# A two-layer hybrid encoder on one core: weight sums by DMA, Strassen blocks on VectorE, and a new order in the last attention head

## The chip, the core and the metric

The kernel runs on one core of a Trainium2 chip. A core has five engines with queues of their own: PE (TensorE, matrix products into PSUM, with PEld for its weight loads), DVE (VectorE), ACT (ScalarE), POOL (GpSimd) and SP (SyncE, which issues DMAs here). The metric is the device time of one execution in microseconds (us), as the median of several runs.

## The reference

768 tokens (a sequence of 512 and one of 256, stored with the shorter one first) go through two layers of width 1024 in float32. Each layer has a mixer and a feed-forward part, each followed by a residual layer norm:

```python
mix = concat([diff_attention(q, k, v, lam), sigmoid(lo) * rmsnorm(mlstm(q2, k2, v2, gates))]) @ w_out
x = layer_norm(ALPHA * x + mix)
gate, up = split(x @ w_gu)                     # 1024 -> 2 x 2816
h = gelu(conv3(gate) + conv_b) * up            # conv3 over neighbouring tokens of one sequence
x = layer_norm(ALPHA * x + h @ w_down)
```

The attention has four heads with two score matrices each, whose softmaxes are subtracted; the mLSTM part runs in both directions with four heads.

## The kernel before

**Precision.** A float32 weight or activation block is split by ACT and DVE into a rounded part (`wh`) and the rest (`wl`, DVE's subtraction in line 187), and every product is three passes on PE. Weights come by SP's queue into six raw buffers (`raw`, line 143), are cast by ACT (line 186) and DVE (line 187), and lie in twelve pairs of slots until PE has read them. The class `Weights` keeps the order of all this: `pump` casts as long as a slot is free, and `_load` issues loads.

**Order.** The code is traced in program order, and a planner writes each engine's instructions out as a fixed list: it takes what is ready by its own clock, the least number first, and `prio(n)` makes the numbers of what it holds smaller by n. A negative n lets the held work stand back. Each engine works its list off in order, so an instruction that waits holds up those behind it.

**Mixer.** Per layer come the mLSTM's inputs and gates, the values, and then per attention head `att_in` (queries and keys, line 379, then casts into `sQ`, `sK`, `kL` by ACT and DVE, lines 722 to 732) and `att` (per tile of 128 queries: scores in lines 752 and 753, the minimum by DVE, the exponential by ACT in line 758, transposes, and the product with the values). Two heads' stages are woven with other work by `weave`. Head 3 handles the sequence of 512 first (`SEQ_ORDER`), but `feat_major` projects the 256 tokens first for every head. In the stage of head 3 the work beside it is the gate projection (`lo`, line 369), its transposes (`loT`), and `split_att` (lines 819 to 825), which casts the outputs of heads 0 to 2 into `actB` for W_out: two ACT copies and two subtractions per head, on POOL for head 0 and on DVE for the others.

**W_out and the change to the FFN.** W_out runs in two column halves over six token tiles. In the second half each tile gets its layer norm: statistics (line 865), aggregate (870), two small steps on POOL (871, 872), and two passes on DVE (876, 882). The FFN's first products use the Strassen-Winograd scheme on 2 x 2 blocks (features by token halves), seven products in place of eight. `combine` (lines 896 to 909) makes the four sums of activations S1 to S4 of a token tile, for tiles 3 and 4 on POOL and for tile 5 on DVE (`VT`), and `to_strassen` transposes and casts them.

**FFN weights.** The scheme also needs four sums of weight blocks per FFN tile f: t1 = u0 + g0, t2 = u1 + t1, t3 = u1 + u0, t4 = g1 + t2. For most tiles SP loads one summand into a buffer `T` (line 152) and POOL issues a DMA that adds the other to it (line 153); four `T` buffers exist, and the next load waits until the cast of the one four earlier was made. For f = 1 and 2 (`ENG`) the raw blocks are loaded, POOL makes t1 and t3, and DVE t2 and t4 (line 164). `ff_tile` (lines 970 to 1010) runs the seven products of a tile, each in one PSUM bank (line 967); DVE reads them out in lines 983 to 999, and a bank is written again when it was read.

**Down projection and end.** `down` (line 1012) adds groups of FFN tiles into `acc`. In the last group the two column halves of a token tile follow each other, DVE adds the product (line 1034), and the layer norm and the output DMA follow (line 1050). For the very last token tiles a part of the norm's last step is done by ACT and POOL (lines 879, 880).

Of the kernel before, what the change touches and what calls it, by code (L numbers as in the profile page):

```python
# [13 lines left out]
F32 = mybir.dt.float32  # L14
# [39 lines left out]
PR_E = 50  # L54
PR_AO = -40
PR_CONV1 = -100
PR_CONV2 = -100
# [28 lines left out]
NSG = 3  # L86
NSUM = 4
ENG = (1, 2)
AT1 = 11
# [4 lines left out]
LAG1 = 2  # L94
VT = (5,)


class Weights:


# [18 lines left out]
    def block(self, src, n, dst=None):  # L119
        self.blocks.append((src, n, dst))  # L120
        for x in (src["a"], src["b"]) if isinstance(src, dict) and src["engine"] else (src,):
            if not isinstance(x, dict):
                self.uses[x] += 1

    def sum(self, layer, a, b, engine=None, over=None):

        s = {"a": a, "b": b, "engine": engine, "layer": layer, "read": False, "over": over}
        if engine is None:
            self.sums.append(s)
        return s  # L130
# [24 lines left out]
    def _value(self, src, n):  # L155
        if isinstance(src, dict):
            if "tile" not in src:

                v = [x["tile"] if isinstance(x, dict) else self.raw[x] for x in (src["a"], src["b"])]
                if isinstance(src["b"], dict) or src["over"]:  # L160
                    src["tile"] = v[1]
                else:
                    src["tile"] = self.diff_pool.tile([128, 512], F32, tag="E", name=f"E{self.n_conv}", bufs=1)
                src["engine"].tensor_tensor(out=src["tile"], in0=v[0], in1=v[1], op=ALU.add)
                for x in (src["a"], src["b"]):
                    if not isinstance(x, dict) and x != src["over"]:
                        self.uses[x] -= 1
            return src["tile"]
        return self.raw[src]

    def _conv(self, i):
        src, n, dst = self.blocks[i]
        self._load()
        v = self._value(src, n)
        if callable(dst):
            dst(v)
            self.uses[src] -= 1
            return
        if dst is None:
            h = self.hl_pool.tile([128, WCOL], F32R, tag="wh", name=f"wh{i}")[:, :n]  # L180
            l = self.hl_pool.tile([128, WCOL], F32R, tag="wl", name=f"wl{i}")[:, :n]
            self.hl[i] = (h, l)
        else:
            h, l = dst
            v = v.rearrange("p (k t) -> p k t", k=4)
        self.nc.scalar.activation(h, v, AF.Identity)  # L186
        self.nc.vector.tensor_tensor(out=l, in0=v, in1=h.bitcast(F32), op=ALU.subtract)  # L187
        if isinstance(src, dict):
            src["read"] = True
            if src["over"]:  # L190
                self.uses[src["over"]] -= 1
        else:
            self.uses[src] -= 1
        self._load()

    def pump(self):

        live = sum(1 for j in range(self.n_done, self.n_conv) if self.blocks[j][2] is None)
        while self.n_conv < len(self.blocks):
            if isinstance(self.blocks[self.n_conv][0], dict):  # L200
                self._load()
                if self.diff_pool is None or ("tile" not in self.blocks[self.n_conv][0] and not self.blocks[self.n_conv][0]["engine"]):
                    break
# [23 lines left out]
def trunk(ctx, nc, tc, d, o, depth=DEPTH):  # L227
# [59 lines left out]
    for l in range(depth):  # L287
# [19 lines left out]
        for kind, i in ffn_seq:  # L307
            if kind == "f":


                def at(w, p):
                    return d[w][l, i, :, p * 512:(p + 1) * 512]

                g0, g1 = early[i] if i in early else [W.piece(at("w_g", p), 512) for p in range(2)]
                if i in ENG:
                    u0, u1 = [W.piece(at("w_u", p), 512) for p in range(2)]
                    t1 = W.sum(l, u0, g0, G)
                    t2 = W.sum(l, u1, t1, V)
                    t3 = W.sum(l, u1, u0, G, over=u0)
                    t4 = W.sum(l, g1, t2, V)  # L320
                else:
                    u1 = W.piece(at("w_u", 1), 512)
                    t1 = W.sum(l, at("w_u", 0), at("w_g", 0))
                    t2 = W.sum(l, at("w_u", 1), t1)
                    t3 = W.sum(l, at("w_u", 1), at("w_u", 0))
                    t4 = W.sum(l, at("w_g", 1), t2)
                for src in (t1, t2, t3, t4, u1) if i in early else (g0, g1, t1, t2, t3, t4, u1):
# [42 lines left out]

    def feat_major(blocks, psA, psB):

        for ps, tok in ((psB, slice(0, SB)), (psA, slice(SB, T))):
            n = 0
# [17 lines left out]
    for l in range(depth):  # L392
# [317 lines left out]
        def att_in(h):  # L710
# [4 lines left out]
            for ui, uu in ((0, uq), (1, uk)):  # L715
                pA = P("d", f"aqkA{h}{ui}")
                pBu = pB[:, ui * 256:(ui + 1) * 256]
                feat_major(uu, pA, pBu)
                W.done(*uu)
                for ps, tk in ((pBu, slice(0, SB)), (pA, slice(SB, T))):  # L720
                    if ui == 0:
# [114 lines left out]

        weave((chain(att_in(3), att(3)), AT3, PR_A), (split_lstm(), 13 - L1 - L2, PR_LO), (chain(*[split_att(h) for h in range(3)]), 4))
        weave((split_att(3), 1))
# [28 lines left out]
        def layer_norm(t, nm, parts=1, aside=()):  # L867
            mv = sm.tile([128, 2], F32, tag="mv", name=f"mv{nm}{t}")
            rs = sm.tile([128, 1], F32, tag="rs", name=f"rs{nm}{t}")
            V.bn_aggr(mv, stats.pop(t))  # L870
            G.tensor_scalar(rs, mv[:, 1:2], EPS, 1.0, op0=ALU.add, op1=ALU.mult)
            G.tensor_tensor(out=rs, in0=rs, in1=mhalf[:, 0:1], op=ALU.pow)
# [97 lines left out]
        def ff_tile(f):  # L970
# [3 lines left out]
            c = ft.tile([128, T], F32, tag="c", name=f"c{f}")  # L974
            m1, u2, u3, u4 = (ft.tile([128, HALF], F32, tag=t, name=f"{t}_{f}") for t in ("m1", "u2", "u3", "u4"))
            lo_, hi_ = slice(0, HALF), slice(HALF, T)
            p1 = bank(f"p1_{f}")
            product(p1, A11)
# [33 lines left out]
        def down(gi):  # L1012
# [5 lines left out]
            for hf, t in ([(hf, t) for t in range(NT) for hf in range(2)] if last else [(hf, t) for hf in range(2) for t in range(NT)]):  # L1018
                if last:
                    units = us[hf]  # L1020
                elif t == 0:
                    units = [W.take() for _ in range(nf)]
                p = P("d" if last else "tu"[(hf * NT + t) % 2], f"dn{gi}{hf}{t}")
                for k, (_, wh_, wl_) in enumerate(units):
                    for i, (a, b) in enumerate(PASSES):
                        x = hm_half((f0 + k) % RING, a, t // 3)[:, (t % 3) * 128:(t % 3 + 1) * 128]
                        PE.matmul(p, x, (wh_, wl_)[b], start=k + i == 0, stop=k == nf - 1 and i == 2)  # L1027
                z = acc[:, t, hf * 512:(hf + 1) * 512]
                if t == NT - 1 and (hf or not last):
                    W.done(*(us[0] + us[1] if last else units))  # L1030
                if gi == 0:
# [3 lines left out]
                if last:  # L1035
                    half_stats(t, hf, f"b{l}")
                if last and hf:
                    final = l == depth - 1
                    parts = 4 if final and t == NT - 1 else 1
                    layer_norm(t, f"b{l}", parts, (() if t < NT - 2 else (0,) if t < NT - 1 else (3,)) if final else ())  # L1040
# [103 lines left out]
```

## Time and profile before

| | us |
|---|---|
| median of 3 runs (1808.42 to 1810.11) | 1808.9 |
| the profiled execution, its own time | 1809.26 |
| its span in the profile | 1807.5 |
| PE busy | 1770.1 |
| DVE busy | 1270.8 |
| ACT busy | 774.5 |
| POOL busy | 273.7 |

The span runs from the first to the last instruction that the profile shows; 1.8 us of the execution lie around it. The mean granted clock of TensorE is 0.997 of full speed. A matmul's recorded duration contains the pipeline behind it, so matmuls that follow each other overlap in the records, and the idle time ahead of one is what counts.

### The profile page before, as it was taken

What the parts mean: (1) busy time and instruction counts of PE and PEld (TensorE: products, weight loads), DVE (VectorE), ACT (ScalarE), POOL (GpSimd) and SP (SyncE); (2) the same over time, 40 slices, a digit from 0 to 9 for tenths busy, and PEclk for the clock granted to TensorE, in tenths of its full rate; (3) what the DMA queues carried; (4) which work ended last, traced back from release to release, by engine and by line L of the source; (5) the groups of instructions that cost most, each with busy time, mean ns of one, the idle gap of its engine ahead of it and who ended that gap; (6) DMA issues with size and microseconds to landing.
All of it is one profiled execution on the core that took longest, in us unless ns stands there. A gap on an engine that the chain in (4) does not pass through costs nothing. (4 is left out here: it accounts for less than half of the span.)

```text
span 1807.5 us, 26787 instructions
## 1 busy us (share of the span) xinstructions
PE 1770.1 (98%) x9692; PEld 1578.8 (87%) x9692; DVE 1270.8 (70%) x2512; ACT 774.5 (43%) x1636; POOL 273.7 (15%) x346
## 2 busy tenths in 40 slices
PE   8999999999999999999999999999999999999998
PEld 8877887889899899899898778878899899898996
DVE  5546887489677577576955468875996676676778
ACT  4445667135334244244323556671453343342340
POOL 2001011241111111110020011102411111111102
PEclk9999999999999999999999999999999999999999
DMA  5312221625666566565232213134356575565631
GB/s 190 101 53 71 73 63 56 189 53 147 143 154 169 121 164 162 124 164 135 88 106 71 62 55 94 48 101 139 76 150 144 129 185 135 134 175 125 155 105 70
DMA packets 129556, 211.55 MB, mean 117 GB/s; under 512 B 12272, under 2 KB 37488, under 8 KB 129424
## 3 DMA queue, kind: packets, MB, share of 16 engines
q1 hardware_dynamic: 105664, 167.51, 29.4%
q0 software_dynamic: 23040, 41.95, 13.9%
q8 instruction: 76, 1.25, 0.3%
q14 instruction: 56, 0.46, 0.1%
q10 hardware_dynamic: 720, 0.37, 0.1%
HBM read 182.43 MB, written 6.39 MB: 104 GB/s over the span
## 5 line engine op out<-in xcount | busy, mean ns | idle before, releaser
L967 PE MATMUL p<-actA,wh 128*128 128x384 f32 x1408 | 362.9, 338 | 0.0
L186 ACT ACTIVATE wh<-raw 128x512 fp32r<-128x512 f32 (+1 forms) x352 | 218.9, 630 | 303.6 <-PE p L967 130.6
L187 DVE TENSOR_TENSOR wl<-raw,wh 128x512 fp32r<-128x512 f32 (+1 forms) x352 | 244.5, 704 | 78.2 <-ACT wh L186 77.6
L967 PE MATMUL p<-actB,wh 128*128 128x384 f32 x1056 | 272.4, 338 | 4.0 <-DVE up L993 3.6
L967 PEld LDWEIGHTS p<-actA,wh 128*128 128x128 f32 x1408 | 254.8, 188 | 1.9 <-DVE acc L926 0.5
L967 PE MATMUL p<-actA,wl 128*128 128x384 f32 x704 | 237.2, 337 | 0.0
L186 ACT ACTIVATE wh<-T 128x512 fp32r<-128x512 f32 x160 | 100.2, 630 | 275.6 <-PE dn L1027 126.0
L1027 PE MATMUL dn<-wh,actB 128*128 128x512 f32 x576 | 207.8, 394 | 0.0
L967 PEld LDWEIGHTS p<-actB,wh 128*128 128x128 f32 x1056 | 192.1, 189 | 5.2 <-DVE up L993 4.3
L1027 PE MATMUL dn<-wh,ring 128*128 128x512 f32 x480 | 178.1, 395 | 0.0
L967 PE MATMUL p<-actB,wl 128*128 128x384 f32 x528 | 177.9, 338 | 0.0
L1034 DVE TENSOR_TENSOR acc<-acc,dn 128x512 f32<-128x512 f32 x144 | 98.3, 685 | 90.6 <-PE dn L1027 90.5
L187 DVE TENSOR_TENSOR wl<-T,wh 128x512 fp32r<-128x512 f32 x160 | 111.8, 705 | 38.2 <-ACT wh L186 38.0
L967 PEld LDWEIGHTS p<-actA,wl 128*128 128x128 f32 x704 | 132.2, 188 | 0.0
L1027 PEld LDWEIGHTS dn<-wh,actB 128*128 128x128 f32 x576 | 108.1, 188 | 25.5 <-ACT actB L1009 0.8
L923 PE MATMUL wo<-wh,actB 128*128 128x512 f32 x384 | 122.9, 397 | 0.0
L153 POOL DMA_DIRECT2D T<-T x80 | 70.0, 875 | 298.4 <-issue 65.0
L1027 PE MATMUL dn<-wl,actB 128*128 128x512 f32 x288 | 113.3, 393 | 0.0
L1027 PEld LDWEIGHTS dn<-wh,ring 128*128 128x128 f32 x480 | 90.2, 188 | 20.7
L153 POOL DMA_DIRECT2D T<-in_w_g_dram x40 | 35.5, 888 | 467.9 <-DMA T<-in_w_u_dram 256.9
L967 PEld LDWEIGHTS p<-actB,wl 128*128 128x128 f32 x528 | 99.7, 189 | 0.0
L1027 PE MATMUL dn<-wl,ring 128*128 128x512 f32 x240 | 94.9, 395 | 0.0
(275 smaller groups left out, 3442.1 us busy)
## 6 DMA issues: line engine op xcount, KB each, us to landing
T<-in_w_u_dram SPq DMA_DIRECT2D x120, 256.0 KB, 2.9
raw<-in_w_g_dram SPq DMA_DIRECT2D x88, 256.0 KB, 3.4
raw<-in_w_down_dram SPq DMA_DIRECT2D x88, 256.0 KB, 3.3
T<-T POOLq DMA_DIRECT2D x80, 256.0 KB, 4.4
raw<-in_w_u_dram SPq DMA_DIRECT2D x48, 256.0 KB, 3.2
T<-in_w_g_dram SPq DMA_DIRECT2D x40, 256.0 KB, 3.9
T<-in_w_g_dram POOLq DMA_DIRECT2D x40, 256.0 KB, 4.6
T<-in_w_u_dram POOLq DMA_DIRECT2D x40, 256.0 KB, 5.8
```

The lines of the kernel that those rows point to most:

```text
L153: self.nc.gpsimd.dma_start(t, s["b"]["tile"] if isinstance(s["b"], dict) else s["b"], accum_op=ALU.add)
L186: self.nc.scalar.activation(h, v, AF.Identity)
L187: self.nc.vector.tensor_tensor(out=l, in0=v, in1=h.bitcast(F32), op=ALU.subtract)
L923: PE.matmul(p, actB[:, k, a, t * 128:(t + 1) * 128], units[k][1 + b], start=n + i == 0, stop=n == 7 and i == 2)
L967: PE.matmul(ps, blk[1 + a][:, k * 128:(k + 1) * 128], x[:, k, b, :], start=k + i == 0, stop=k == 3 and i == 2)
L1027: PE.matmul(p, x, (wh_, wl_)[b], start=k + i == 0, stop=k == nf - 1 and i == 2)
L1034: V.tensor_tensor(out=z, in0=z, in1=p, op=ALU.add)
```

## The change

- `ENG` and the engine sums are gone: all four sums of every FFN tile come by a load and an accumulating DMA, and the `T` buffers grow from four to six (`NSUM`).
- The Strassen sums of activations of tiles 3, 4 and 5 are all made by DVE (`VT`).
- `att_in` projects queries and keys in the order in which the head attends, so head 3 projects the 512 tokens first and casts them first.
- `split_att` of heads 0, 1 and 2 is traced behind head 3's first, second and third query tile, and stands back by 40 (`PR_SPL`).
- The first of the layer norm's two small POOL steps goes to DVE.
- The FFN temporaries u2 and u3 share memory with m1 and with half of g.
- The very last output piece (token tile 5, second column half) is computed in two column halves with separate statistics, and token tile 4's last norm step is cut in two, the first half on ACT and POOL, the second on DVE.

```diff
+PR_SPL = -40
-NSUM = 4
-ENG = (1, 2)
+NSUM = 6
-VT = (5,)
+VT = (3, 4, 5)
...
     def _value(self, src, n):
-        if isinstance(src, dict):
-            if "tile" not in src:
...
-                src["engine"].tensor_tensor(out=src["tile"], in0=v[0], in1=v[1], op=ALU.add)
...
+        return src["tile"] if isinstance(src, dict) else self.raw[src]
...
-                if i in ENG:
-                    u0, u1 = [W.piece(at("w_u", p), 512) for p in range(2)]
-                    t1 = W.sum(l, u0, g0, G)
-                    t2 = W.sum(l, u1, t1, V)
-                    t3 = W.sum(l, u1, u0, G, over=u0)
-                    t4 = W.sum(l, g1, t2, V)
-                else:
...
+                u1 = W.piece(at("w_u", 1), 512)
+                t1 = W.sum(l, at("w_u", 0), at("w_g", 0))
+                t2 = W.sum(l, at("w_u", 1), t1)
+                t3 = W.sum(l, at("w_u", 1), at("w_u", 0))
+                t4 = W.sum(l, at("w_g", 1), t2)
...
-    def feat_major(blocks, psA, psB):
-        for ps, tok in ((psB, slice(0, SB)), (psA, slice(SB, T))):
+    def feat_major(blocks, parts):
+        for ps, tok in parts:
...
-                feat_major(uu, pA, pBu)
+                parts = [{0: pBu, 2: pA}[s0] for s0, _ in SEQ_ORDER[h]]
+                parts = [(ps, slice(0, SB) if ps is pBu else slice(SB, T)) for ps in parts]
+                feat_major(uu, parts)
                 W.done(*uu)
-                for ps, tk in ((pBu, slice(0, SB)), (pA, slice(SB, T))):
+                for ps, tk in parts:
...
-        weave((chain(att_in(3), att(3)), AT3, PR_A), (split_lstm(), 13 - L1 - L2, PR_LO), (chain(*[split_att(h) for h in range(3)]), 4))
+        def att_split(h):
+            for i, _ in enumerate(att(h)):
+                if i < h:
+                    with prio(PR_SPL):
+                        for _ in split_att(i):
+                            pass
+                yield
+        weave((chain(att_in(3), att_split(3)), AT3, PR_A), (split_lstm(), 13 - L1 - L2, PR_LO))
...
-            G.tensor_scalar(rs, mv[:, 1:2], EPS, 1.0, op0=ALU.add, op1=ALU.mult)
+            V.tensor_scalar(rs, mv[:, 1:2], EPS, 1.0, op0=ALU.add, op1=ALU.mult)
...
-            m1, u2, u3, u4 = (ft.tile([128, HALF], F32, tag=t, name=f"{t}_{f}") for t in ("m1", "u2", "u3", "u4"))
+            m1, u4 = (ft.tile([128, HALF], F32, tag=t, name=f"{t}_{f}") for t in ("m1", "u4"))
+            u2, u3 = m1, g[:, hi_]
...
+                very = last and hf and t == NT - 1 and l == depth - 1
+                cut = [slice(0, 256), slice(256, 512)] if very else [slice(0, 512)]
...
+                            PE.matmul(p[:, cs], x, (wh_, wl_)[b][:, cs], start=k + i == 0, stop=k == nf - 1 and i == 2)
+                if very:
+                    st = sm.tile([128, 3, 6], F32, tag="bs3", name="bs3", bufs=1)
+                    V.tensor_copy(st[:, 0, :], stats[t][:, 0, :])
+                    for i, (p, cs) in enumerate(zip(ps, cut)):
+                        z = acc[:, t, 512 + cs.start:512 + cs.stop]
+                        V.tensor_tensor(out=z, in0=z, in1=p[:, cs], op=ALU.add)
+                        V.bn_stats(st[:, 1 + i, :], z)
+                    stats[t] = st
...
-                    parts = 4 if final and t == NT - 1 else 1
+                    parts = 4 if final and t == NT - 1 else 2 if final and t == NT - 2 else 1
```

## Rows read from the trace of the kernel before

**Rows 1.** The page: its head, and part 1 for PE (busy us, share).

```profile
span 1807.5 us, 26787 instructions
...
PE 1770.1 (98%) x9692; PEld 1578.8 (87%) x9692; DVE 1270.8 (70%) x2512; ACT 774.5 (43%) x1636; POOL 273.7 (15%) x346
```

**Rows 2.** Who PE waited for: us in total, times, longest one.

```profile
PE aoT L781 <- DVE ao L776: 3.9, 6, 1.0
PE p L967 <- DVE up L993: 3.6, 2, 1.8
PE s L752 <- ACT sK L729: 3.1, 2, 1.6
PE aoT L781 <- DVE cc L759: 1.6, 2, 0.8
...
PE y0T L386 <- DVE actA L389: 0.6, 1, 0.6
...
PE y1T L386 <- DVE actA L389: 0.6, 1, 0.6
```

**Rows 3.** Timeline of ACT, layer 1, head 3 (start us, us, line, operation).

```profile
1173.91 2.57 ACT L823 CAST actB<-av 128x256 fp32r<-128x256 f32 x6
```

**Rows 4.** Timeline of PE, same stretch; in brackets the idle time before.

```profile
1174.51 0.39 PE L379 MATMUL aqkA<-actA,wl 128*128 128x512 f32 x1
...
1178.72 0.50 PE L752 MATMUL s<-sK,sQ 128*128 128x512 f32 x1 [1.54 <-ACT sK L729]
```

**Rows 5.** Windows of line 379 alone: stretch, length, PE busy (matmuls), PEld, clock.

```profile
1163.50:1165.10 1.60, 1.58 (x13) 1.55 (x13) 1.00 0.50 146
1169.00:1174.90 5.90, 5.80 (x24) 4.42 (x24) 1.00 0.00 0
```

**Rows 6.** Line 824: count, shortest/median/longest ns, first and last start.

```profile
L824 POOL TENSOR_TENSOR actB<-av,actB x4: 734/1016/1297, 277.8 to 1175.1; 128x256 fp32r<-128x256 f32 x2, 128x512 fp32r<-128x512 f32 x2
```

**Rows 7.** Timeline of DVE, layer 1, second half of W_out and first FFN tiles.

```profile
1280.12 2.50 DVE L187 TENSOR_TENSOR wl<-T,wh 128x512 fp32r<-128x512 f32 x2
...
1289.40 0.68 DVE L905 TENSOR_TENSOR S<-acc 128x512 f32<-128x512 f32 x1
...
1304.44 4.06 DVE L187 TENSOR_TENSOR wl<-raw,wh 128x512 fp32r<-128x512 f32 x3
1308.42 0.55 DVE L993 SCALAR_TENSOR_TENSOR up<-p,u 128x384 f32<-128x384 f32 x1
```

**Rows 8.** Timeline of POOL, same stretch.

```profile
1280.34 1.73 POOL L907 TENSOR_TENSOR S<-acc 128x512 f32<-128x512 f32 x1
...
1286.04 0.88 POOL L871 TENSOR_SCALAR rsa<-mva 128x1 f32<-128x1 f32 x1
...
1304.61 1.66 POOL L164 TENSOR_TENSOR E<-raw,raw 128x512 f32<-128x512 f32 x1 [4.35 <-DVE wl L187]
1306.35 1.60 POOL L164 TENSOR_TENSOR raw<-raw,raw 128x512 f32<-128x512 f32 x1
```

**Rows 9.** Windows: length, PE, PEld, DVE, ACT, POOL busy (x), granted clock, DMA.

```profile
1264.90:1297.40 32.50, 31.72 (x185) 26.95 (x184) 28.89 (x43) 14.75 (x26) 17.23 (x17) 1.00 0.19 42
1306.00:1309.70 3.70, 1.86 (x11) 1.55 (x10) 3.70 (x5) 0.87 (x2) 1.87 (x2) 1.00 0.47 142
1309.70:1313.10 3.40, 3.40 (x12) 3.40 (x11) 3.37 (x7) 1.09 (x2) 0.00 (x0) 0.50 0.02 5
1313.10:1319.00 5.90, 5.90 (x35) 5.90 (x35) 3.38 (x7) 3.80 (x6) 0.00 (x0) 1.00 0.00 0
```

**Rows 10.** Line 153, POOL's accumulating DMAs: shortest/median/longest ns, and issue to landing.

```profile
L153 POOL DMA_DIRECT2D T<-T x80: 859/874/900, 337.1 to 1736.3; - x80
...
DMA to landing us min/median/max: 3.2/4.7/7.5
```

**Rows 11.** Timeline of all engines, the end.

```profile
1798.97 0.69 DVE L1034 TENSOR_TENSOR acc<-acc,dn 128x512 f32<-128x512 f32 x1 [0.71 <-PE dn L1027]
...
1800.67 2.03 DVE L876 SCALAR_TENSOR_TENSOR acc<-acc,mvb,lng 128x256 f32<-128x256 f32 x4
```

More of the change, by code (lines that the diff above doesn't have):

```diff
@@ L120, in block, with sum @@
         self.blocks.append((src, n, dst))
[L121 to L129, printed above, removed]
+        if not isinstance(src, dict):
+            self.uses[src] += 1
+    def sum(self, layer, a, b):
+        s = {"a": a, "b": b, "layer": layer, "read": False}
+        self.sums.append(s)
         return s
@@ L155, in _value @@
     def _value(self, src, n):
-        if isinstance(src, dict):
-            if "tile" not in src:
-                v = [x["tile"] if isinstance(x, dict) else self.raw[x] for x in (src["a"], src["b"])]
-                if isinstance(src["b"], dict) or src["over"]:
-                    src["tile"] = v[1]
-                else:
-                    src["tile"] = self.diff_pool.tile([128, 512], F32, tag="E", name=f"E{self.n_conv}", bufs=1)
-                src["engine"].tensor_tensor(out=src["tile"], in0=v[0], in1=v[1], op=ALU.add)
[L165 to L169, printed above, removed]
+        return src["tile"] if isinstance(src, dict) else self.raw[src]
     def _conv(self, i):
@@ L189, in _conv @@
             src["read"] = True
-            if src["over"]:
-                self.uses[src["over"]] -= 1
         else:
@@ L201, in pump @@
                 self._load()
-                if self.diff_pool is None or ("tile" not in self.blocks[self.n_conv][0] and not self.blocks[self.n_conv][0]["engine"]):
+                if self.diff_pool is None or "tile" not in self.blocks[self.n_conv][0]:
                     break
@@ L314, in trunk @@
                 g0, g1 = early[i] if i in early else [W.piece(at("w_g", p), 512) for p in range(2)]
-                if i in ENG:
-                    u0, u1 = [W.piece(at("w_u", p), 512) for p in range(2)]
-                    t1 = W.sum(l, u0, g0, G)
-                    t2 = W.sum(l, u1, t1, V)
-                    t3 = W.sum(l, u1, u0, G, over=u0)
-                    t4 = W.sum(l, g1, t2, V)
[L321 to L326, printed above, removed]
+                u1 = W.piece(at("w_u", 1), 512)
[3 more added lines that the diff above has]
+                t4 = W.sum(l, at("w_g", 1), t2)
                 for src in (t1, t2, t3, t4, u1) if i in early else (g0, g1, t1, t2, t3, t4, u1):
@@ L1022, in down @@
                     units = [W.take() for _ in range(nf)]
[L1023 to L1027, printed above, removed]
+                very = last and hf and t == NT - 1 and l == depth - 1
+                cut = [slice(0, 256), slice(256, 512)] if very else [slice(0, 512)]
+                ps = [P("d" if last else "tu"[(hf * NT + t) % 2], f"dn{gi}{hf}{t}{i}") for i in range(len(cut))]
+                for p, cs in zip(ps, cut):
+                    for k, (_, wh_, wl_) in enumerate(units):
+                        for i, (a, b) in enumerate(PASSES):
+                            x = hm_half((f0 + k) % RING, a, t // 3)[:, (t % 3) * 128:(t % 3 + 1) * 128]
+                            PE.matmul(p[:, cs], x, (wh_, wl_)[b][:, cs], start=k + i == 0, stop=k == nf - 1 and i == 2)
[7 more added lines that the diff above has]
+                    stats[t] = st
                 z = acc[:, t, hf * 512:(hf + 1) * 512]
@@ L1030, in down @@
                     W.done(*(us[0] + us[1] if last else units))
-                if gi == 0:
+                if very:
+                    pass
+                elif gi == 0:
                     V.scalar_tensor_tensor(out=z, in0=z, scalar=ALPHA, in1=p, op0=ALU.mult, op1=ALU.add)
@@ L1034, in down @@
                     V.tensor_tensor(out=z, in0=z, in1=p, op=ALU.add)
-                if last:
+                if last and not very:
                     half_stats(t, hf, f"b{l}")
```

## The prediction

> **What bounds the kernel now.** I read the page first: PE is busy for 98% of a span of 1807.5 us [rows 1]. Little is to be had except where PE stands still. The list of PE's waits says where: apart from the start and the end, the waits are a few tenths to 1.8 us each, and they lie in two stages that occur once per layer. In the stage of attention head 3, PE's first score product waits for the last cast of the keys (3.1 us in two waits), and later the transposes of the attention output wait for DVE (1.6 us of the 5.5 us under that line have DVE's line 759 as releaser, and these two belong to head 3). At the change from W_out to the FFN, the transposes of the Strassen blocks wait for a DVE cast (0.6 us in each layer), and the first FFN tile's fifth product waits for the DVE reading that frees its bank, line 993 (3.6 us in two waits) [rows 2].
>
> I then read these stages in time. In head 3 of layer 1, the projection of keys over the long sequence ends with a matmul at 1174.51, and the score product starts at 1178.72 after 1.54 us of idle time [rows 4]. In between ACT runs six casts of finished attention heads, 2.57 us, ahead of the key casts [rows 3]. At the FFN, three casts on DVE take 4.06 us from 1304.44 on, and line 993 comes only at 1308.42 [rows 7]. An undisturbed 128x512 operation with two SBUF inputs takes 0.68 us on the same engine [rows 7], so three are worth 2.0 us; the other 2.0 us fall just where POOL runs the two weight sums of line 164, 1.66 and 1.60 us [rows 8]. The two casts at 1280.12 show the same: 2.50 in place of 1.36 us while POOL makes a Strassen block in 1.73 us [rows 7, 8]. So the operations that the change takes from POOL hold DVE up. Last, the granted clock falls to half from 1309.7 for 3.4 us, right behind a stretch in which PE was busy for 1.86 of 3.70 us; 12 matmuls went through there, and the stretch behind it gives 35 in 5.9 us, 0.169 each [rows 9]. The drop cost about 3.4 - 12 x 0.169 = 1.4 us, in layer 1 alone.
>
> **The change part by part.**
> *Weight sums of FFN tiles 1 and 2 by DMA.* Removed are, per layer, four sums on POOL and four on DVE (DVE's 0.68 us each) and two raw loads; added are eight loads on SP and eight accumulating issues on POOL. POOL's issue takes 0.87 us and lands 4.7 us later, 7.5 at worst [rows 10]. With six buffers the first two new sums start with the first four, long before use. The third needs the first buffer read, by the casts that start at 1280.12 and end at 1282.6 [rows 7]; load and accumulation at twice the worst landing and one issue make 1298.5. The second tile wants it two products behind the stall at 1308.42, so over 10 us are left and the sums cost PE nothing; without that slack, a late landing would cost a wait of its own size. What goes is the 2.0 us stretch of DVE, and with it the wait: -3.6 us, and the 1.4 us of the clock. What is late next is the same DVE reading, now some 0.7 us or more ahead of PE's need.
>
> *All Strassen blocks on DVE.* Tiles 3 and 4 add eight operations per layer: 8 x 0.68 = 5.4 us. The stretch of 32.5 us that holds them has 28.89 us of DVE work, so 3.6 us idle [rows 9]; the disturbed casts give 1.1 us back. 5.4 - 1.1 - 3.6 = 0.7 us too much per layer, and the small operation that the layer norm moves from POOL to DVE (one column, four times) adds a little: I take 0.8 us of new wait per layer, 1.6 in all. Ends: 0, because some of the weight casts there can be put off, and 4.3 per layer if none of the idle time can be used. Against it the waits of the transposes (0.6 twice, [rows 2]) go, since tile 3's blocks are ready earlier: -1.2 us.
>
> *Attended sequence first in head 3.* Queries and keys over 512 tokens are now projected ahead of those over 256. A 256-column matmul takes 1.58 / 13 = 0.12 us and a 512-column one 5.80 / 24 = 0.24 [rows 5], so 24 of the short ones, 2.9 us, now cover the casts of the long keys. Every matmul and cast of the projection stays. The wait of 1.54 us is shorter than the cover: -3.1 us.
>
> *Casts behind query tiles.* Six ACT casts, four DVE casts and two POOL casts per layer move in among the query tiles of head 3, where ACT has the exponentials to do. POOL's two, 0.73 and 1.30 us [rows 6], now fall beside attention work on DVE; a stretched DVE operation there costs up to 1.1 us, as the one at 1280.12 did, or nothing where PE still has gate projections to run. I take nothing for it (ends 0 and 2.2 us), and for the new order one wait per layer of the kind that the transposes now have, 3.9 / 6 = 0.65 us [rows 2]: +1.3 us. The attention chain starts earlier, and of the 1.6 us at its end I take half: -0.8 us (ends 0 and 1.6).
>
> *End of the kernel.* Twelve 512-column matmuls become 24 of 256: 24 x 0.12 - 12 x 0.24 = 0 from the rows. Behind the last one, an addition and a statistic of 0.69 us each shrink to the size of the 256-wide operations, 2.03 / 4 = 0.51 us: -0.4. But DVE gets half of tile 4's last step (0.68, taken from ACT and POOL), the first half's addition and statistic (1.0) and two tiny ones, and had only 0.71 us idle there [rows 11]: up to +1.0 us. I take +0.4, since part of it can run while PE works on the second half; ends -0.4 and +1.0. Sharing the buffers of two FFN temporaries adds no wait, since the same engine writes and reads them in the same order.
>
> *Sum:* -3.1 - 0.8 - 3.6 - 1.2 - 1.4 + 1.6 + 1.3 + 0.4 = -6.8 us. The profiled execution took 1809.3 us, which gives 1802.5; the median of the runs shown is 0.4 us lower, which gives 1802.1; I say 1802.3. About 0.2%, 3.6 us, is what a measurement of this kernel can tell from no change.
>
> **Rivals.** (a) *Given back in head 3.* The casts still need ACT's 2.57 us somewhere in the stage; if the chain of exponentials on ACT is what PE really follows, the 3.1 and 0.8 us come back as waits at scores or transposes. For it: PE waits for that chain again at the stage's end [rows 2]. Against it: PE has the gate projection to fill in. -6.8 + 3.9 = -2.9: 1806.2.
>
> (b) *Slower: DVE becomes the bound at the FFN.* The place is the first product that reads a Strassen block. It decides if DVE cannot use its 3.6 us of idle time [rows 9], because that time lies ahead of tile 4 and the load behind it. Then PE waits 4.3 us per layer in place of 0.8 (+7.0), the transposes' 1.2 us are not gained, and a standstill longer than the one that halved the clock halves it in both layers, 1.4 us each: 2.8 more than forecast. -6.8 + 7.0 + 1.2 + 2.8 = +4.2: 1813.3. Against it: tile 3's blocks fall where DVE waits for POOL now.
>
> (c) *POOL's queue.* The layer norm's power stays on POOL. If a new accumulation stands ahead of it and waits for its load, tile 5's norm is late: the buffer is free at 1282.6, a landing takes 4.7 us and an issue 0.87 [rows 10], which makes 1288.2, while POOL's steps of that norm start at 1286.04 now [rows 8]. That is 2.2 us per layer, 4.4 in all: 1806.7. The Trainium skill (SBUF — State Buffer, "SBUF: two separate sides") warns that a DMA issued from GpSimd is starved while VectorE holds the port pair that both share, 620 ns growing to 3100. By that rule two issues ahead of the power would add about 5 us per layer and the result would be near 1817. The 80 issues of this trace spread only from 859 to 900 ns beside a DVE that is 70% busy [rows 1, 10], so this form of the rival gets 2 in 100 at most.
>
> **How the numbers follow.** The forecast gets 0.64, (a) 0.16, (b) 0.10, (c) 0.10. The forecast's own range is 1797 to 1805: all ends on the good side (1.6 instead of 0.8, no new waits, -0.4 at the end) give 1809.3 - 11.3 = 1798.0, less the median's 0.4; the new terms doubled (3.3 us more) give the other end. To 1808 it takes in (a) and most of (c). Faster by over 0.2% needs 1805.3 or less: 0.68, the forecast and a little of (a); within 0.2%: 0.22; slower: 0.10, which is (b).
>
> **What would show it.** Right: no POOL sums and no DVE operation beside them over 0.7 us at the first FFN tiles; line 993 no longer among PE's releasers; PE's scores in head 3 behind the short key projection without a wait; no half clock near 1310. A little new idle time of PE, under 1 us, ahead of the first product on a Strassen block. Wrong: the same total of PE's waits in the attention stage under other names (a); over 3 us of PE idle at the first Strassen product, with DVE without a pause before it (b); DVE waiting for POOL's power while POOL waits for a load (c).

## The result and the profile after

| | before | after |
|---|---|---|
| median of the runs | 1809.3 us (1808.4 to 1810.1, 4 runs) | 1830.4 us (1829.3 to 1832.7, 4 runs) |
| ratio, with its 95% interval | | 1.0114 [1.0102, 1.0126] |
| span of the profiled execution | 1807.5 us | 1827.5 us |

The change makes the kernel 1.1% slower, 21 us, where 7 us less had been forecast. The profile's span grew by 20.0 us. Its head and its line for PE answer to [rows 1]:

```profile
span 1827.5 us, 26990 instructions
...
PE 1774.9 (97%) x9704; PEld 1582.3 (87%) x9704; DVE 1270.7 (70%) x2549; ACT 779.5 (43%) x1636; POOL 256.4 (14%) x314
```

PE is busy for only 4.8 us more, so some 15 us are standstill. Line numbers have shifted: 967 is now 954 (the FFN product), 983 and 993 are 971 and 981 (readouts of its banks), 187 and 186 are 171 and 170 (the weight casts on DVE and ACT), 153 is 150 (POOL's accumulating DMA). The list of PE's waits answers to [rows 2] (engine, line, whom it waited for: us in total, times, longest):

```profile
PE p L954 <- DVE g L971: 10.8, 2, 6.0
...
PE p L954 <- DVE up L981: 5.3, 2, 2.9
...
PE s L731 <- DVE kL L709: 2.3, 2, 1.2
PE u L746 <- DVE aT L744: 2.1, 2, 1.1
PE aoT L759 <- DVE den L642: 2.0, 2, 1.0
PE aoT L759 <- DVE cc L737: 2.0, 2, 1.0
PE p L954 <- ACT actA L363: 1.9, 4, 0.7
```

The FFN's first products wait 16.1 us for the DVE readouts that free their banks, 3.6 before: 12.5 us more, in two waits per layer. The waits around head 3 are others, and more (below). The waits of the transposes fell from 0.6 us in each layer to 0.3 and 0.2, but the products behind them now wait for ACT's casts of the same blocks, 1.9 us and in the next line of the kind 0.7, where before had 0.3: 1.6 us more together.

The windows over those two waits in layer 1 answer to [rows 9] (stretch, length, busy time and count of PE, PEld, DVE, ACT, POOL, then the granted clock and the DMA share):

```profile
1317.00:1320.70 3.70, 2.12 (x13) 1.80 (x11) 1.83 (x3) 2.50 (x5) 0.89 (x1) 1.00 0.91 176
1320.70:1324.10 3.40, 2.09 (x7) 2.09 (x8) 2.75 (x6) 0.67 (x2) 0.87 (x1) 0.63 1.06 290
1324.10:1331.80 7.70, 5.65 (x30) 5.33 (x29) 2.54 (x5) 2.07 (x3) 2.78 (x4) 0.94 0.88 196
1331.80:1338.60 6.80, 4.02 (x13) 4.02 (x14) 4.88 (x8) 4.92 (x8) 1.09 (x2) 0.50 0.94 240
```

With each of these two waits the clock drops to its lower level (1.2 in place of 2.4 GHz). The last stretch pushes 13 matmuls through in 4.02 us, which take 13 x 0.169 = 2.2 us at full clock by the rate of [rows 9]; the second has 7 in 2.09 us in place of 1.2, and the third still holds the end of that drop (0.06 x 7.70 = 0.5 us lost). Layer 0 has one such stretch:

```profile
420.80:423.90 3.10, 0.00 (x0) 0.00 (x0) 2.21 (x4) 2.07 (x3) 1.74 (x2) 0.99 0.69 165
423.90:430.70 6.80, 3.92 (x12) 3.92 (x13) 5.21 (x9) 4.83 (x7) 1.02 (x2) 0.50 0.97 232
```

That is 12 in 3.92 us in place of 2.0. Half clock costs 1.8 + 0.9 + 0.5 + 1.9 = 5.1 us, 1.4 before: 3.7 us more. With the 12.5 us of waits, 2.2 us around head 3 (below) and 1.6 at the transposes this makes the 20.0 us by which the span grew. Waits of tenths, which went both ways, are left out, so the agreement is good to about 1 us and no better.

**Why DVE reads the banks late.** Its timeline in that stretch, where [rows 7] had three casts and then the readout (start, duration, operation; in brackets the idle time before and what ended it):

```profile
1318.87 0.69 DVE L171 TENSOR_TENSOR wl<-T,wh 128x512 fp32r<-128x512 f32 x1 [2.38 <-ACT wh L170]
1319.47 2.01 DVE L171 TENSOR_TENSOR wl<-raw,wh 128x512 fp32r<-128x512 f32 x3
1321.40 0.55 DVE L981 SCALAR_TENSOR_TENSOR up<-p,g 128x384 f32<-128x384 f32 x1
...
1322.94 0.55 DVE L987 SCALAR_TENSOR_TENSOR up<-p,u 128x384 f32<-128x384 f32 x1
1329.12 1.29 DVE L171 TENSOR_TENSOR wl<-T,wh 128x512 fp32r<-128x512 f32 x2 [5.63 <-ACT wh L170]
...
1333.37 0.69 DVE L171 TENSOR_TENSOR wl<-T,wh 128x512 fp32r<-128x512 f32 x1 [0.61 <-ACT wh L170]
1333.98 0.55 DVE L971 TENSOR_TENSOR g<-p,m 128x384 f32<-128x384 f32 x1
```

The three casts of raw blocks now take 2.01 us, not 4.06: nothing of POOL stretches them any more, as forecast. But DVE stands idle for 2.38 and 5.63 us in front of casts whose rounded halves ACT has not made, and the readouts stand behind these casts in DVE's list. ACT waits for the sums:

```profile
1318.20 0.63 ACT L170 ACTIVATE wh<-T 128x512 fp32r<-128x512 f32 x1 [3.96 <-DMA T<-T]
...
1319.78 0.46 ACT L967 COPY m<-p 128x384 f32<-128x384 f32 x1
...
1328.45 1.16 ACT L170 ACTIVATE wh<-T 128x512 fp32r<-128x512 f32 x2 [7.08 <-DMA T<-T]
...
1332.71 0.63 ACT L170 ACTIVATE wh<-T 128x512 fp32r<-128x512 f32 x1 [2.19 <-DMA T<-T]
```

The first of PE's two waits ends with line 981 at 1321.40, which had only such casts ahead of it. The second, for line 971, has one link more. Line 971 at 1333.98 needs a product that ended long before, the copy `m`, which ACT finished at 1319.78 + 0.46 = 1320.24, and the buffer `g`, of which there is only one: the tile before must have been convolved. That takes a step on ACT and then four on DVE:

```profile
1329.51 1.01 ACT L988 ACTIVATE c<-g,convw 128x768 f32<-128x768 f32 x1
```

```profile
1330.55 1.15 DVE L990 SCALAR_TENSOR_TENSOR c<-g,convw,c 128x255 f32<-128x255 f32 x2
1331.62 1.14 DVE L991 SCALAR_TENSOR_TENSOR c<-g,convw,c 128x255 f32<-128x255 f32 x2
```

DVE had written the last part of that `g` by 1323.0 and was free at 1323.5; it reached line 971 10.5 us later. ACT's step could have run at 1323.0 too, but stood 6.5 us behind the two late casts in ACT's list. By the durations shown line 971 could have started near 1323.0 + 1.0 + 2.2 = 1326.2 (an estimate), before PE stood still at 1329.7. So the same late casts hold the readout up in two lists, ACT's and DVE's. The weights that it waited for are those of FFN tile 2 (the tenth to twelfth sums, counted from the casts), and PE takes the first of that tile's sums only here:

```profile
1344.93 0.51 PE L954 MATMUL p<-actB,wh 128*128 128x384 f32 x2
```

So PE did not wait for weights: it waited for a bank whose readout stood in DVE's list behind the cast of a weight that nobody needed yet.

**Why the sums are late.** POOL's timeline, all of it accumulating DMAs:

```profile
1308.89 0.92 POOL L150 DMA_DIRECT2D T<-in_w_u_dram  x1 [9.58 <-DVE actB L364]
1312.69 0.87 POOL L150 DMA_DIRECT2D T<-T  x1 [2.88 <-DVE wl L171]
...
1317.53 0.89 POOL L150 DMA_DIRECT2D T<-in_w_u_dram  x1 [1.91 <-DMA T<-in_w_u_dram]
1321.03 0.87 POOL L150 DMA_DIRECT2D T<-T  x1 [2.60 <-DMA T<-in_w_g_dram]
1324.53 0.86 POOL L150 DMA_DIRECT2D T<-in_w_g_dram  x1 [2.63 <-DMA T<-in_w_u_dram]
1328.99 0.86 POOL L150 DMA_DIRECT2D T<-T  x1 [3.60 <-DMA T<-in_w_g_dram]
```

Each is issued when the load or the sum that it needs has landed, and they are issued in one order. t2 adds t1, and t4 adds t2, so three landings follow each other in each tile: the cast of tile 1's last sum starts at 1318.20, 5.5 us after its issue at 1312.69; tile 2's t2 is issued at 1321.03 and cast at 1328.45, its t4 at 1328.99 and 1332.71. A landing is no longer than before, 3.2/4.6/8.0 us (shortest, median, longest) against 3.2/4.7/7.5 [rows 10]. All this starts late: the buffers come free with DVE's casts of the first sums, which ran at 1280.12 before [rows 7] and now run from here on:

```profile
1304.82 0.68 DVE L171 TENSOR_TENSOR wl<-T,wh 128x512 fp32r<-128x512 f32 x1
```

11 of these 25 us are the shift that layer 0 and head 3 had caused by then (the FFN's first product starts at 1293.5 in place of 1282.5); 14 are the casts' own delay, in which DVE makes the Strassen blocks. The first experiment, which gives the blocks back to POOL, shows it: there the first of these casts is at 1291.72, 2.4 us ahead of the FFN's first product, just as before.

### The profile page after: what moved, and what is told of

It reads as the page before. It is cut to its first block, busy times and chain, and to the rows that moved or that the text cites. A ratio compares the mean times of both kernels' runs of the same rounds, so it can differ in the third digit from the quotient of the medians.

```text
span 1827.5 us, 26990 instructions
## 1 busy us (share of the span) xinstructions
PE 1774.9 (97%) x9704; PEld 1582.3 (87%) x9704; DVE 1270.7 (70%) x2549; ACT 779.5 (43%) x1636; POOL 256.4 (14%) x314
## 4 chain that ended last, share of the span: by engine, by line
PE 85%; DVE 6%; DMA 3%; ACT 2%; issue 2%; POOL 1%; SPq 0%; POOLq 0%; ACTq 0%; DVEq 0%
PE p L954 34%; PE dn L1019 19%; PE wo L910 6%; PE aqkA L354 4%; PE av L344 3%; PE lv L344 3%; PE lo L344 2%; PE c1a L344 2%; PE aqkB L354 2%; PE c1b L344 2%; PE u L746 2%; PE s L730 1%; PE s L731 1%; DMA T<-T 1%; PE aT L742 1%
## 5 line engine op out<-in xcount | busy, mean ns | idle before, releaser
L171 DVE TENSOR_TENSOR wl<-raw,wh 128x512 fp32r<-128x512 f32 (+1 forms) x348 | 237.0, 690 | 84.7 <-ACT wh L170 83.9
L170 ACT ACTIVATE wh<-T 128x512 fp32r<-128x512 f32 x176 | 111.1, 633 | 297.1 <-PE p L954 134.3
L1019 PE MATMUL dn<-wh,ring 128*128 128x512 f32 (+1 forms) x484 | 178.4, 393 | 0.0
L171 DVE TENSOR_TENSOR wl<-T,wh 128x512 fp32r<-128x512 f32 x176 | 119.6, 689 | 36.1 <-ACT wh L170 36.0
L150 POOL DMA_DIRECT2D T<-T x88 | 76.6, 870 | 272.0 <-DMA T<-in_w_g_dram 76.6
L150 POOL DMA_DIRECT2D T<-in_w_u_dram x44 | 39.4, 894 | 414.7 <-DMA T<-in_w_u_dram 211.3
L1019 PE MATMUL dn<-wl,ring 128*128 128x512 f32 (+1 forms) x242 | 95.2, 393 | 0.0
```

The lines of the kernel that those rows point to most:

```text
L150: self.nc.gpsimd.dma_start(t, s["b"]["tile"] if isinstance(s["b"], dict) else s["b"], accum_op=ALU.add)
L1019: PE.matmul(p[:, cs], x, (wh_, wl_)[b][:, cs], start=k + i == 0, stop=k == nf - 1 and i == 2)
```

## The experiments

Each is timed beside the kernel before on the same chip (1809.6 to 1810.2 us); "ratio" is to that.

**Two rivals for the cause.** Theory 1: VectorE's new Strassen blocks put off the casts that free the buffers. Theory 2: the sums of the first tiles by DMA are too slow as such. The blocks go back to POOL, in the kernel after:

```diff
-VT = (3, 4, 5)
+VT = (5,)
```

> The change with one constant set back: the Strassen blocks of tiles 3 and 4 are made by POOL again (VT = (5,)). Theory 1 (displaced casts): the eight block operations on DVE put off the weight casts that free the first sum buffers from 1280 to 1305 us in layer 1, so the loads and accumulations of the sums of FFN tiles 1 and 2 start 25 us late; with the blocks on POOL the first buffer is read before 1290, the two PE waits of 2.6 to 6.1 us per layer and the half clocks go, and the time is 1812 to 1818. Rival 2 (the DMA sums of the first tiles are too slow whoever makes the blocks): over 8 us of waits per layer stay, 1825 to 1831.

Measured 1825.6 us, ratio 1.0086 [1.0071, 1.0102]: 5 us better, 16 worse than before. POOL's timeline in layer 1:

```profile
1296.66 0.92 POOL L150 DMA_DIRECT2D T<-in_w_u_dram  x1
...
1309.14 0.89 POOL L150 DMA_DIRECT2D T<-in_w_g_dram  x1 [10.07 <-ACT actA L363]
1315.13 0.89 POOL L150 DMA_DIRECT2D T<-T  x1 [5.10 <-ACT wh L170]
```

Tile 1's sums are now issued from 1296.66 on and are in time. Tile 2's follow from 1309.14 and are late, and the wait of `p` behind line 971 is still 11.0 us in two, while that behind line 981 is gone. The time lies in the range of theory 2, and theory 1 alone (1812 to 1818) is out: the displaced casts explain about a quarter of the loss. In layer 1 PE also waits 1.3 us for the copy `m`, which stands behind casts of late sums in ACT's list.

**The engines' sums back,** for f = 1 and 2, in the kernel after (four buffers; `Weights.sum` and `_value` as before):

```diff
-NSUM = 6
+NSUM = 4
+ENG = (1, 2)
```

> The change with the weight sums of FFN tiles 1 and 2 made by POOL and DVE again (four sum buffers), the blocks still on DVE. Theory 1: the casts of the first sum buffers are still late (after 1300 us), but no DMA chain hangs on them before FFN tile 3, so the long waits go: 1812 to 1819. Rival 3 (DVE alone is the bound at the FFN, with or without DMA sums): PE still waits 4 us or more per layer there, 1822 or more. Rival 2 agrees with theory 1 here.

Measured 1812.3 us, ratio 1.0012 [1.0003, 1.0022], with a mean granted clock of 0.999 in place of 0.994. 18 of the 21 us are the sums, with their two further buffers. The blocks are still on DVE here, so DVE's total work is not the bound either (1822 or more had been expected for that).

**Head 3 undone,** in the kernel after: projection order and `split_att` as before.

```diff
-parts = [{0: pBu, 2: pA}[s0] for s0, _ in SEQ_ORDER[h]]
+parts = [{0: pBu, 2: pA}[s0] for s0, _ in SEQS]
...
-weave((chain(att_in(3), att_split(3)), AT3, PR_A), (split_lstm(), 13 - L1 - L2, PR_LO))
+weave((chain(att_in(3), att(3)), AT3, PR_A), (split_lstm(), 13 - L1 - L2, PR_LO), (chain(*[split_att(h) for h in range(3)]), 4))
```

> The change without its part in attention head 3 (256 tokens projected first again, casts of the finished heads woven in as before). By the traces the stage of head 3 lost 2.5 us in layer 0 and 3.1 in layer 1 with the change: theory 1 with that reading expects 1824 to 1826. Rival: the part gains its 3 us as forecast and other work in the stage lost them; then the time stays at 1830 or rises to 1834.

Measured 1829.5 us, ratio 1.0113 [1.0096, 1.0129], not to be told from after's, and above the 1824 to 1826 that the length of the stage in the traces had led me to expect. In this kernel head 3's part is no large cost, and no gain either.

**The casts sooner,** in the kernel after: the number by which weight casts stand back in W_out.

```diff
-PR_CONV1 = -100
+PR_CONV1 = -10
```

> The change with the weight casts of this stage standing back by 10 in place of 100 (PR_CONV1 = -10), so that they come ahead of the Strassen blocks in the planner's order. DVE's work is the same. Theory 1: the first buffers are read before 1290, the sums are in time, and the two long waits shrink; the blocks are late instead, so PE waits up to 3 us at the first product on a block: 1814 to 1824. Rival 3 (DVE's total is the bound): 1826 to 1832, the wait only moves.

Measured 1838.6 us, ratio 1.0159 [1.0144, 1.0174], worse, and above both ranges. The edit did not do what it was meant for: the first cast of a sum on DVE is at 1312.67, 11.3 us behind the FFN's first product (1301.3), as in the kernel after (1304.82 and 1293.5). So the run does not try theory 1. Once they start, the casts now go ahead of those of the activations, and PE waits for these:

```profile
PE p L954 <- DVE g L971: 6.9, 2, 4.3
PE p L954 <- DVE up L981: 4.7, 2, 2.7
...
PE y0T L361 <- DVE actA L364: 3.3, 2, 3.0
PE y1T L361 <- DVE actA L364: 3.2, 2, 2.9
```

**One tile each.** First only f = 2's sums by the engines, then only f = 1's, in the kernel after with its six buffers:

```diff
+ENG = (2,)
```

> The kernel after, with the sums of weight tile f = 2 alone made by the engines again (as before); those of f = 1 stay with the DMAs, and six buffers T. Theory (two causes: f = 2's four sums by DMA come late whatever is done, since their buffers are freed only by f = 1's casts and two of them hang in a chain; f = 1's are late only because of that list's order of casts): most of the loss goes, 1812 to 1818 us, ratio 1.002 to 1.005; the wait of p behind DVE g (10.8 us in after) falls below 5. Rival (the first tile's sums by DMA, after VectorE's blocks put off the casts that free the buffers, are the loss): 1822 to 1828, as in the run with the blocks on GpSimd but from the other side, with the wait staying above 8 us.

```diff
+ENG = (1,)
```

> The kernel after, with the sums of weight tile f = 1 alone made by the engines; f = 2's stay with the DMAs, which now have f = 1's two spare buffers and its time to land. Theory (a sum by DMA is late only where its buffer is freed by casts less than some 25 us ahead of its use, and f = 2's sums now take buffers T4 to T7): 1812 to 1818, the readouts of the banks no longer behind casts that wait for a DMA, no half clock. Rival (three tiles' worth of accumulating DMAs in series on one queue are too slow in themselves): the wait moves to f = 2, 1820 to 1828, with half clock in one stretch per layer at least.

Measured 1816.3 us, ratio 1.0031 [1.0020, 1.0041], with f = 1 by DMA, as expected; and 1808.8 us, ratio 0.9990 [0.9980, 0.9999], with f = 2 by DMA, better than either range. The second one's PE is busy throughout the stretch that was broken, with the clock at full:

```profile
1303.00:1337.00 34.00, 34.00 (x196) 34.00 (x195) 31.69 (x58) 20.11 (x34) 9.39 (x11) 1.00 0.97 237
```

Its buffers come free no sooner. They are loaded from 1299.47 on, 13 us behind the FFN's first product at 1286.1; in the kernel after it was 12 (1305.57 less 1293.5). But two of tile 2's four sums lie in the two spare buffers by then, and the other two have one tile more of time. So the expectation's first reason, that tile 2's sums come late whatever is done, was wrong: they come late when tile 1's stand ahead of them for the buffers. Against the run with both by the engines (1812.3), tile 2's by DMA gain 3.5 us, and tile 1's by DMA lose 4.0; both together lose 18.2. (The run with both by the engines had four buffers and another chip, so the 3.5 and 4.0 are good to a microsecond or two; by the ratios they are 4.0 and 3.4.) That the two sets queue for the same two spare buffers fits all four runs; the number of buffers was not varied by itself.

**The casts inside the FFN put back further,** in the kernel after:

```diff
-PR_CONV2 = -100
+PR_CONV2 = -300
```

> The kernel after, with one number changed: the priority of the weight casts inside the FFN (PR_CONV2) goes from -100 to -300, which orders other work of VectorE and ScalarE against them. If the casts that wait for a DMA stand ahead of the readouts that free the banks because of this number (theory), the order on VectorE changes and the time moves by more than 3 us either way: down to about 1824 if readouts come ahead, up by as much if still more casts go ahead of them. Rival (the loss is TensorE waiting for the weights themselves, not for banks): within 2 us of after, 1828 to 1832.

Measured 1831.9 us, ratio 1.0116 [1.0101, 1.0131]. This run decides nothing: the planner wrote the same instructions in the same order on every engine. The planner ranks by that number only among what it takes to be ready, so the casts are ahead of the readouts because by its own clock the sums had landed; that last step is inferred and not shown. It serves as a second measurement of the kernel after.

**Single parts on the kernel before.** Head 3's part alone (the diff of the run on head 3, the other way round):

> The kernel before with one part of the change alone: head 3's projection order and the casts behind the query tiles. From the trace of after, where that stage is 2.5 and 3.1 us longer than in before: 1810 to 1814, ratio 1.001 to 1.003. By my prediction's term (3.1 + 0.8 us saved): 1805 to 1807.

Measured 1813.2 us, ratio 1.0019 [1.0009, 1.0028]: slower by 3.5 us. PE's waits around that stage, and then, from the same list of the kernel before, the one that was not shown yet:

```profile
PE s L756 <- DVE kL L734: 2.3, 2, 1.2
PE u L771 <- DVE aT L769: 2.1, 2, 1.1
PE aoT L784 <- DVE cc L762: 2.0, 2, 1.0
PE aoT L784 <- DVE den L668: 2.0, 2, 1.0
```

```profile
PE u L768 <- DVE aT L766: 1.5, 2, 0.8
```

They are the same four as in the kernel after and make 8.4 us, where before had 3.1 + 1.6 + 1.5 = 6.2 [rows 2]. The two at `u` and at `den` come while PE still works on head 3's projection: in layer 1 of the kernel after they end at 1175.18 and 1178.87, ahead of head 3's first score at 1185.92.

The Strassen blocks on VectorE alone:

```diff
-VT = (5,)
+VT = (3, 4, 5)
```

> The kernel before with one part of the change alone: the Strassen blocks of stages 3 and 4 on VectorE in place of GpSimd. With the engines' sums in place, by my prediction's price (a new wait of some 0.8 us per layer, no late sums but those of f = 1 and 2): 1808 to 1812. If putting off the casts alone already costs TensorE the FFN's start (theory 1): over 1814.

Measured 1814.3 us, ratio 1.0026 [1.0015, 1.0036]: 4 us slower, just over the bound that had been set for theory 1. DVE, its casts put off, waits for a sum that POOL makes late:

```profile
1314.71 1.22 DVE L187 TENSOR_TENSOR wl<-E,wh 128x512 fp32r<-128x512 f32 x1 [2.22 <-ACT wh L186]
```

PE's wait behind line 983 is 5.4 us in two, 3.6 and 1.8, and the clock halves in both layers. The end of the kernel alone (the last output piece in column halves, tile 4's last norm step in two parts, and the norm's small step on VectorE):

> The kernel before with one part of the change alone: the last output piece in column halves, the norm of the last tile but one in two parts, and the norm's first small operation on VectorE. From the stretch behind the last full product (8.5 us in before, 8.2 in after): within 0.5 us of before, ratio 0.9995 to 1.0005. By my prediction's term for the end (0.4 us lost): 1809 to 1811.

Measured 1809.5 us, ratio 0.9997 [0.9987, 1.0007]: nothing that can be told.

**A version that beats both.** The kernel after with f = 1's sums by the engines and head 3 as before (its `weave` as in the run on head 3):

```diff
+ENG = (1,)
...
-parts = [{0: pBu, 2: pA}[s0] for s0, _ in SEQ_ORDER[h]]
+parts = [{0: pBu, 2: pA}[s0] for s0, _ in SEQS]
```

> The kernel after with two parts taken back: f = 1's sums made by the engines, and head 3's projection order and casts as before. Theory (head 3's part costs 3.5 us by itself, as where it stood alone on before, and adds to the rest): 1808.8 - 3.5 = 1805.3, between 1804 and 1807, ratio 0.997 to 0.9985. Rival (its cost is hidden or replaced once the FFN's wait is gone, as it was only 1 us in the kernel after): 1807 to 1809.

Measured 1806.3 us, ratio 0.9974 [0.9964, 0.9984]. And the same with the blocks of tiles 3 and 4 on POOL (`VT = (5,)`):

> As the run before it, with the Strassen blocks of the stages 3 and 4 on GpSimd again as in before, so that VectorE's casts come early. If VectorE's blocks are a cost wherever they stand ahead of the casts (theory 1): 1 to 4 us below that run, f = 2's sums earlier. If VectorE has room for them and what they gain is that its operations no longer run beside GpSimd's (the 1.75 against 0.69 us of one subtraction): equal or 1 to 3 us above it.

Measured 1804.7 us, ratio 0.9970 [0.9958, 0.9982]. Both beat the kernel before, by 0.26 and 0.30%. Their intervals overlap, so where the blocks are best made stays open. Neither has a wait at the FFN's readouts among PE's larger ones.

Eight buffers, which would give both tiles spare ones, were not tried. Nor was a list in which the readouts, and ACT's step of the convolution, stand ahead of the casts, nor a second buffer `g`. So that the order in the lists of DVE and ACT turns a late sum into PE's wait is read from the timeline, and not from a run that changes it alone.

## Why the prediction was wrong

**The step that failed** is the slack of the third new sum: "load and accumulation at twice the worst landing and one issue make 1298.5 ... over 10 us are left and the sums cost PE nothing; without that slack, a late landing would cost a wait of its own size". Three things in it were wrong. It started from casts at 1280.12, and the blocks that the same change gives to DVE put these off by 14 us; I had costed the blocks only as DVE's time, not as a delay of the casts that free the buffers. It counted one load and one accumulation for one sum, where only two of the eight sums of two tiles have a spare buffer, the others wait for buffers one after the other, and each tile has three landings in series. And it priced lateness as a wait of PE for the weight, on the tile that uses it. The landings themselves were inside the bound: 8.0 us at worst, where twice 7.5 had been allowed.

**The price of lateness** was not a wait of its own size where it is due, but a wait elsewhere: DVE and ACT stand in front of the late casts, and what stands behind them holds PE's banks, though the weights are needed 10 us and more later. The term -3.6 for the FFN's waits became +12.5. The -1.4 for the clock became +3.7: more drops, and longer ones. These two terms are off by 16.1 + 5.1 = 21.2 us, most of the 28 between 1802.3 and 1830.4; head 3 (4.8) and the transposes (2.8) come next, as the next parts show. The +1.6 for the blocks and the +0.4 for the end have no wait of their own in the rows after, which takes 2.0 off.

**The wait of the kernel before** was misread in one point: it is not the first tile's fifth product that waits at 1309.02. 110 matmuls of line 967 start ahead of that wait, nine products of twelve and two more, so all of the first tile is through and the one that waits belongs to the second.

**Head 3** (-3.1 - 0.8 + 1.3 = -2.6) became +2.2 by the waits, +3.5 by the run of that part alone. The mechanism was half right: the first product on the rounded keys no longer waits, but the next one, on the rest `kL`, does. PE's timeline of the kernel after, which answers to [rows 4], and DVE's beside it:

```profile
1185.92 0.48 PE L730 MATMUL s<-sK,sQ 128*128 128x512 f32 x1
1187.56 0.50 PE L731 MATMUL s<-kL,sQ 128*128 128x512 f32 x1 [1.16 <-DVE kL L709]
```

```profile
1184.37 1.14 DVE L655 SCALAR_TENSOR_TENSOR hq<-hq,rsl,lstmg 128x128 f32<-128x128 f32 x4 [1.84 <-POOL rsl L652]
1186.22 0.69 DVE L364 TENSOR_TENSOR actB<-loT,actB 128x512 fp32r<-128x512 f32 x1 [0.71 <-ACT actB L363]
1186.82 0.68 DVE L709 TENSOR_TENSOR kL<-aqkA,sK 64x512 fp32r<-64x512 f32 x1
```

The first `kL` (line 709) needs the first of ACT's casts of the keys, done at 1183.55, but starts 3.3 us later. In DVE's list it stands behind a step of the mLSTM, for which DVE waited 1.84 us on POOL, and behind the cast of the gate's transposes shown: again a list held up by what stands first. 24 short matmuls of cover were worked out from [rows 5] and were there; the chain they covered had a second link. The new waits at `u` and `aoT` are those for which I took 1.3 us for the new order: 8.4 - 2.3 = 6.1 against 3.1 before, 3.0 in place of 1.3. Rival (a), that it is given back in this stage, had the sign right here and was too mild; its reason, ACT's chain of exponentials, is not what the rows show, since all four waits end with a step of DVE. The cost is not the same beside every other part either: 3.5 us alone on the kernel before, 1.0 us (not to be told from nothing) in the kernel after.

**The blocks on DVE** were the new wait of 0.8 us per layer, and rival (b) the same with more. Alone they cost 4 us. Rival (b)'s +4.2 is a sum over the whole change and can't be set beside this; its own price for the blocks was a wait of 4.3 us per layer, and the run shows 3.6 and 1.8 us behind line 983, where before had 1.8 in each layer behind line 993 [rows 2]. Its half clock in both layers came. But the place was another: the wait is at the readouts, not at the first product on a block. Rival (b) had the right engine and the wrong queue position, and its price did not hold for the sums.

**POOL's queue,** rival (c): POOL never holds the norm's power for a load: the new sums start only when the norms are over (their last power is at 1297.9, the first late sum at 1308.89), and all 76 us of POOL's waits in front of the first norm's power are put down to DVE's step before it. As to the rule of the Trainium skill (SBUF — State Buffer, "SBUF: two separate sides") that a DMA issued from GpSimd starves while VectorE runs an operation in a 2-port mode, which locks the ports that both share (a condition that the prediction left out), the 176 issues of the kernel after took between 859 and 1242 ns with DVE 70% busy:

```profile
L150 POOL DMA_DIRECT2D T<-T x88: 859/868/1062, 338.6 to 1745.5; - x88
```

No run here shows the stall of the kind that it describes, and the loss is not of that kind: POOL waits for landings, not for its ports.

**The transposes** (-1.2) gave 0.7, and the products behind them took 2.3 more: the wait moved on to the next reader, ACT's casts of the transposed blocks, so that the term came out at +1.6.

**Right** was DVE without POOL's stretch (2.01 us for three casts). The end of the kernel is within 0.1% of nothing; the +0.4 can be told neither from that nor from a small gain. **Sharing the buffers** of the FFN temporaries was not tried alone. The reason given, that one engine writes and reads them, is wrong for `m1`, which ACT writes; but where ACT's copy comes late in the kernel after, at 1319.78, DVE's last step on the shared buffer had ended at 1316.49, and the copy stood behind a late cast.

## What to carry to other kernels

Where each engine works off a fixed list, a late operand costs not where it is used but wherever the instruction that touches it first stands: before making a transfer later, look at what is queued behind its first reader on that engine, and put work that frees PSUM banks ahead of it, with every step that this work waits for on other engines (that this helps is a conclusion from the timeline; no run here tried it). Slack for a prefetched chain has to be counted from the instruction that frees its buffer in the changed order, with every landing in series, for all tiles that share the buffers. And a change that moves work onto one engine and makes something else depend on that engine's promptness should be costed together: tile 1's sums by DMA lost 4 us, both tiles' 18, and tile 2's alone gained 3.5.

## What was not expected of the hardware

- The norm's power on POOL, one column, takes 0.55 to 0.57 us in 23 of 24 cases in the kernel before, and 1.45 to 1.54 in 21 of 24 after (the others 0.65, 0.92 and 1.40). The run of the end alone, which also moves the small step ahead of it to DVE, shows it too. The first row is before's, the second after's, each for half of the cases:

```profile
L872 POOL TENSOR_TENSOR rsa<-rsa,mhalf x12: 548/557/571, 355.0 to 1287.0; 128x1 f32<-128x1 f32 x12
```

```profile
L859 POOL TENSOR_TENSOR rsa<-rsa,mhalf x12: 1449/1517/1538, 354.8 to 1297.9; 128x1 f32<-128x1 f32 x12
```

In the kernel before the step that was taken away took 0.19 us in 13 of 24 cases and 0.25 to 1.28 in the others (0.88 in [rows 8]). So POOL's part of a norm, 0.74 us in those 13, did not become shorter by giving the step away, but longer. The cause was not tried.
- An operation of DVE with two SBUF inputs takes 1.2 to 1.8 us while POOL runs one of its own, and 0.68 without (1.77 us for the second cast of the pair at 1280.12 [rows 7, 8], 1.22 in the run of the blocks alone). Taking POOL's operations away restored the 0.68 fully, and the kernel gained nothing by it, since the three casts then waited for something else.
- The clock's drop does not follow the length of the wait alone: in the kernel after, a standstill of 2.4 us in layer 0 brought no drop, one of 2.9 us in layer 1 brought 3.4 us at the lower level, and those of 6.0 and 4.8 us brought 6.8 us each; in the kernel before, two of 1.8 us brought none in layer 0 and 3.4 us in layer 1.
